# A hybrid RWKV-7 and latent-attention block: rotary parts of queries and key on GpSimd, and one PSUM bank copied out before a norm

## The chip, the cores and the metric

The kernel runs on one core of one Trainium2 chip, in one launch. A NeuronCore has five engines that each work through an instruction list of their own, in order: TensorE (PE in the profile, with PEld for its weight loads), VectorE (DVE), ScalarE (ACT), GpSimd (POOL) and SyncE (SP, which issues most of the loads). They meet only through semaphores. TensorE writes PSUM banks; the others work in SBUF and, all but GpSimd here, in PSUM. The metric is device time in microseconds for one execution of the program; the time of a kernel is the median of its runs.

## What is computed

One residual block over 256 tokens, width 2048, all float32. Cut to what matters here:

```python
u = rms_norm(h, pre_mix_norm)
z_rw, z_mla, z_gate = jnp.split(u @ w_in, ...)
y_rw = rwkv7_mixer(z_rw, ...)               # 16 heads x 64, state scan over time
cq, ckv, k_pe = jnp.split(z_mla, (512, 1024), axis=-1)
q  = (rms_norm(cq, q_norm) @ w_q_up).reshape(B, S, 8, 192)     # 128 plain + 64 rotary per head
kv = (rms_norm(ckv, kv_norm) @ w_kv_up).reshape(B, S, 8, 256)  # 128 key + 128 value per head
def rope(x, cos, sin):
    x1, x2 = jnp.split(x, 2, axis=-1)
    return jnp.concatenate([x1 * cos - x2 * sin, x2 * cos + x1 * sin], axis=-1)
q_pe = rope(q_pe, ...); k_pe = rope(k_pe, ...)                 # one key part for all heads
y_mla = block_causal_softmax(q, k) @ v
mix = (sigmoid(gA) * (y_rw @ Wa) + sigmoid(gB) * (y_mla @ Wb)) @ W_out
h = h + rms_norm(mix); h = h + rms_norm(gated_conv_mlp(h)); h = h + rms_norm(sigmoid(h @ W_pg) * (p @ W_ple))
```

The rotary step takes each vector of 64, swaps its two halves, and adds the original times cosine and the swapped one times plus or minus sine. The block needs it for eight query heads (four tiles of 128 rows: two heads in each) and for the one key part.

## The kernel before

**Products.** Activations are kept feature by feature: 128 features on the partitions, 256 tokens along the row. To keep float32 accuracy, each operand is cut into a high half (`hi`, rounded to the engine's fast float32 form) and a low half (`lo`, what is left), and three products are added: hi x hi, hi x lo, lo x hi (`fm3`, L183, L184, L185; `tm` with L196, L198 and L200 where tokens become the rows of the result, as for the values). A weight chunk is 128 x 1024 floats, 512 KB, loaded by SyncE into one of three `raw` buffers; `wchunk` cuts it in two steps of 512 columns, ScalarE making `hi` (L148) and VectorE making `lo` (L149), with five buffers of each. So every chunk that TensorE uses costs ScalarE two casts and VectorE two subtractions. A "duo" is a product with two times 128 output features into one PSUM bank (`d`); four such banks go round.

**The first 120 us.** Duos 1 to 4 of the input projection give the query latent and the key/value latent, each of 512 features. `latent` copies them out and sums their squares; `latent_norm` makes the reciprocal root on VectorE, spreads it over the partitions with two transposes on TensorE (`rs`, L377), scales each of the four 128-feature blocks (`latn`, L409) and splits the result into halves (`latm`, L161 on ScalarE and L162 on VectorE). Between them come a narrow product with the low-rank columns and the rotary key, and duos 0 and 5, the first RWKV parts; they are copied out by `evac` (L354), scaled by `rsb` (L368) and mixed with the token before (`rw_mix`, L361 and L362). Duo 5 is the last that uses `uT` without its norm factor; then `u_part` rewrites `uT` in four parts (L600 on VectorE, then L161 and L162), for all later RWKV duos.

Then come two duos with the rotary rows of the queries (w_q chunks 4 and 5), four value chunks (`dv0`, `dv1`, four times), the plain query and key duos of heads 0 and 1 (`upo`), and the attention of eight heads, two at a time, woven with further query, key and RWKV duos. The scores (`sc`) add a plain product (L637) and a rotary one (L638, `qp` with `kpe`).

**The rotary parts.** The query duo is copied to `o` (a tile named `upo`); ScalarE copies its four 32-partition quarters into `b` (`qps`) with neighbours exchanged (L610); VectorE multiplies `b` by sine (L612) and `o` by cosine into `a` (`qp`, L613) and adds (L614). For the key, VectorE writes the product with cosine into 64 partitions of each of two tiles `kpe` whose other halves are zero (L584), four products with minus sine into 32 partitions of `kp2` each (L586), and two sums (L588). The sign of sine for the first halves was folded into `sinT` before (L574).

**What sets the order.** The kernel's lines are recorded once; a tile framework then gives each engine its list, when the program is built, by priorities: lines written earlier go first where they can, the copies out of PSUM (`evac`, `rw_mix`) are raised, and work like `u_part` fills places in between. Engines never reorder at run time. Tiles of one tag share buffers in turn: `e1` has 5 of 256 columns and `e2` 17 of 512, and a new tile waits until the former owner of its buffer has been read for the last time. `kp2` takes the buffer of the broadcast `rb` of the second latent norm, which the transposes L377 read.

Of the kernel before, what the change touches and what calls it, by code (L numbers as in the profile page):

```python
# [11 lines left out]
AF = mybir.ActivationFunctionType  # L12
ALU = mybir.AluOpType
# [3 lines left out]
P = 128  # L17
T = 256
# [90 lines left out]
def hybrid_block(tc, A):  # L109
    nc = tc.nc  # L110
    es = ExitStack()
    mm = nc.tensor.matmul
    act = nc.scalar.activation
    tt = nc.vector.tensor_tensor
    ts = nc.vector.tensor_scalar
    stt = nc.vector.scalar_tensor_tensor

# [197 lines left out]
    def e1(nm, shape=None, dt=F32):  # L315
        return mp.tile(shape or [P, T], dt, name=nm, tag="e1", bufs=5)

    def e2(nm, shape=None, dt=F32):
        return mp.tile(shape or [P, 2 * T], dt, name=nm, tag="e2", bufs=17)
# [11 lines left out]
    def win_duo(i, ahead=None):  # L331
        return dense(umov, [A["w_in"][i, q] for q in range(4)], 4, ahead)

    def run(g):

        while True:
            try:
                next(g)
            except StopIteration as e:
                return e.value  # L340
# [11 lines left out]
    def evac(out, ps, **k):  # L352
        with tc.high_priority():
            act(out, ps, AF.Copy, **k)  # L354
# [8 lines left out]
                    op0=ALU.mult, op1=ALU.add)  # L363


    def scaled(out, ps, nb=2):
        evac(out, ps)
        tt(out=out, in0=out, in1=rsb[:].unsqueeze(1).to_broadcast([P, nb, T]), op=ALU.mult)  # L368

    def bcast(col, dst):  # L370
# [125 lines left out]
    cosT = mp.tile([P, T], F32, name="cosT")  # L496
    sinT = mp.tile([P, T], F32, name="sinT")
# [36 lines left out]
    lora = xn[:, 0, 0:3 * T].rearrange("p (b t) -> p b t", b=3)  # L534
    LM = zp.tile([P, 7, T], F32R, name="LM", bufs=1)
    akv = latent(lat[2:4])
    ps = run(dense(umov, [A["w_in1"][q] for q in range(2)], 8, cols=(0,)))
    rsb = mp.tile([P, T], F32, name="rsb")
    bcast(st[:, 6:8], rsb[:])
    cq = latent_norm(*aq, "q_norm")  # L540
    zs = e2("zs", [P, 2, T])
    scaled(zs[:, 0:1, :], ps[:, 0:1, :], 1)
    rw_mix(zs, 2, lora[:, 2:3, :], 1)
    zs = e2("zs", [P, 2, T])
    ps = run(win_duo(0))
# [1 line left out]
    rw_mix(zs, 0, lora[:, 0:2, :])  # L547

    zs = e2("zs", [P, 2, T])
    ps = run(win_duo(5))  # L550
    ckv = latent_norm(*akv, "kv_norm")
    scaled(zs[:], ps[:])
    zz = [[zp.tile([P, 2, T], F32, name="z0")], [], [], []]
    rw_mix(zs, 3, zz[0][0])
    act(lora[0:64, 0, :], lora[0:64, 0, :], AF.Tanh)
# [16 lines left out]
    Q = [slice(32 * i, 32 * i + 32) for i in range(4)]  # L572
# [5 lines left out]
    kpe = [mp.tile([P, T], F32, name=f"kpe{i}") for i in range(2)]  # L578
    kp2 = e1("kp2")
    key = lora[64:128, 2, :]  # L580
    for i in range(2):
        p = slice(64 * i, 64 * i + 64)
        nc.gpsimd.memset(kpe[i][64 - 64 * i:128 - 64 * i, :], 0.0)
        tt(out=kpe[i][p], in0=key, in1=cosT[64:128], op=ALU.mult)  # L584
        for x in range(2):
            stt(out=kp2[Q[2 * i + 1 - x]], in0=lora[Q[2 + x], 2, :], scalar=-1.0, in1=sinT[Q[2 + x]],  # L586
                op0=ALU.mult, op1=ALU.mult)
        tt(out=kpe[i][p], in0=kpe[i][p], in1=kp2[p], op=ALU.add)  # L588

    def up2(ap, lat):  # L590

# [13 lines left out]
    for j in range(2):  # L605
        ps = run(dense(cq, [A["w_q"][4 + j]], 4))
        o, b = e2("upo", [P, 2, T]), e2("qps", [P, 2, T])
        evac(o[:], ps[:])
        for i in range(4):
            act(b[Q[i ^ 1]], o[Q[i]], AF.Copy)  # L610
        a = mp.tile([P, 2, T], F32, name=f"qp{j}")
        tt(out=b[:], in0=b[:], in1=sinT[:].unsqueeze(1).to_broadcast([P, 2, T]), op=ALU.mult)  # L612
        tt(out=a[:], in0=o[:], in1=cosT[:].unsqueeze(1).to_broadcast([P, 2, T]), op=ALU.mult)  # L613
        tt(out=a[:], in0=a[:], in1=b[:], op=ALU.add)  # L614
        qp += [a[:, c, :] for c in range(2)]

    vt = [e2("vt") for _ in range(4)]
# [600 lines left out]
    with tc.tile_pool(name="fw", bufs=2) as fw, tc.tile_pool(name="psu", bufs=3, space=PSUM, reuse_waits="tile") as psu:  # L1218
# [30 lines left out]
        for n, (j, q) in enumerate([(j, q) for q in range(4) for j in range(3)] + [(j, q) for j in range(3, NFF) for q in range(4)]):  # L1249
            if q == 0:  # L1250
                pu[j] = psu.tile([P, 2, 512], F32, name="d")
            ps = pu[j]
# [193 lines left out]
```

## Time and profile before

| what | value |
|---|---|
| time, median of 3 runs | 1560.78 us (1560.56 to 1561.42) |
| profiled execution: time, span | 1560.39 us, 1558.6 us |
| TensorE busy, granted clock | 1538.0 us (99%), 0.997 |
| VectorE busy | 1182.2 us (76%) |
| ScalarE busy | 942.1 us (60%) |
| GpSimd busy | 60.9 us (4%) |
| loads | 281.16 MB read, 182 GB/s over the span |

The profiled execution's time is 1.8 us above its span, which runs from the first to the last instruction. Busy shares are means over the whole span; stages within it differ, and VectorE is much busier near 100 us than on average. In the profile's rows, a group reads: line, engine, operation, names of what it writes and reads, shape, count, then busy us and mean ns of one, then the engine's idle time before them and what ended it. A row of the timeline begins with start and length in us. Two operations of VectorE overlap by some 0.08 us in their recorded lengths when they run back to back.

### The profile page before, as it was taken

To read this page: it belongs to the slowest core of one execution; us is meant where nothing else is said; L and a number is where in the kernel's file an instruction comes from. 1 tells how busy PE (TensorE), PEld (TensorE's weight loads), DVE (VectorE), ACT (ScalarE), POOL (GpSimd) and SP (SyncE) were. 2 spreads that over 40 slices of the span, in tenths; PEclk is the share of its full clock that TensorE was granted. 3 is DMA by queue.
4 is the path that set the end of the run, shared out by engine and by line. 5 is a ranking of instruction groups with operands and counts; after the bars stand their busy time and mean duration, and the time that the engine had idled before them with its cause. 6 is when DMAs were issued, how large, how long until landed. Compare 5 with 4: busy or idle time off the path is not lost.

```text
span 1558.6 us, 29636 instructions
## 1 busy us (share of the span) xinstructions
PE 1538.0 (99%) x10850; PEld 1388.3 (89%) x10850; DVE 1182.2 (76%) x2670; ACT 942.1 (60%) x1944; POOL 60.9 (4%) x125
## 2 busy tenths in 40 slices
PE   9999999999999999999999999999999999999997
PEld 9989999999999999887888888888888888888886
DVE  7896687898989776557787777777777655777866
ACT  7686756566565555456766555555655555776653
POOL 0000201101011102000000000000000000000000
PEclk9999999999999999999999999999999999999998
DMA  8654555454444546865656555565655666666564
GB/s 304 192 172 141 154 173 164 138 171 129 147 150 136 160 153 200 306 199 167 203 174 205 198 181 202 179 203 179 206 181 190 175 192 195 197 197 191 166 200 148
DMA packets 80482, 285.19 MB, mean 183 GB/s; under 512 B 9040, under 2 KB 10320, under 8 KB 80336
## 3 DMA queue, kind: packets, MB, share of 16 engines
q1 hardware_dynamic: 77760, 279.48, 56.3%
q10 hardware_dynamic: 2576, 3.81, 0.7%
q8 instruction: 85, 1.39, 0.4%
q14 instruction: 61, 0.50, 0.1%
HBM read 281.16 MB, written 2.10 MB: 182 GB/s over the span
## 4 chain that ended last, share of the span: by engine, by line
PE 89%; DVE 6%; ACT 2%; DMA 1%; issue 1%; DVEq 0%; ACTq 0%
PE d L170 21%; PE d L174 11%; PE d L183 9%; PE d L185 8%; PE d L184 8%; PE o L196 7%; PE o L198 6%; PE o L200 6%; PE e L196 2%; PE e L198 2%; PE e L200 2%; DVE lo L149 2%; ACT hi L148 1%; DMA raw<-in_w_in 1%; PE tr L237 0%
## 5 line engine op out<-in xcount | busy, mean ns | idle before, releaser
L149 DVE TENSOR_TENSOR lo<-raw,hi 128x512 fp32r<-128x512 f32 x684 | 461.0, 690 | 213.9 <-ACT hi L148 208.5
L148 ACT CAST hi<-raw 128x512 fp32r<-128x512 f32 x684 | 410.7, 619 | 297.9 <-PE o L200 97.9
L183 PE MATMUL d<-uT,hi 128*128 128x256 f32 x1072 | 307.7, 287 | 0.7 <-ACT hi L161 0.6
L170 PE MATMUL d<-u,highs 128*128 128x512 f32 x1312 | 305.5, 390 | 0.0
L185 PE MATMUL d<-uT,lo 128*128 128x256 f32 x1072 | 300.5, 280 | 0.7 <-DVE lo L162 0.2
L184 PE MATMUL d<-uT,hi 128*128 128x256 f32 x1072 | 299.6, 279 | 0.1
L170 PEld LDWEIGHTS d<-u,highs 128*128 128x128 f32 x1312 | 243.3, 188 | 48.9
L148 ACT CAST highs<-raw 128x512 fp32r<-128x512 f32 x328 | 186.8, 616 | 115.0 <-DMA raw<-in_w_up 80.3
L183 PEld LDWEIGHTS d<-uT,hi 128*128 128x128 f32 x1072 | 201.7, 188 | 2.8 <-ACT hi L161 0.8
L185 PEld LDWEIGHTS d<-uT,lo 128*128 128x128 f32 x1072 | 201.5, 188 | 2.1 <-DVE lo L149 1.1
L184 PEld LDWEIGHTS d<-uT,hi 128*128 128x128 f32 x1072 | 201.7, 188 | 0.4 <-DVE uT L290 0.3
L149 DVE TENSOR_TENSOR hi<-raw,highs 128x512 fp32r<-128x512 f32 x164 | 112.7, 688 | 76.8 <-PE d L174 58.8
L174 PE MATMUL d<-u,lo 128*128 128x256 f32 x752 | 117.7, 280 | 0.0
L149 DVE TENSOR_TENSOR lo<-raw,highs 128x512 fp32r<-128x512 f32 x164 | 112.0, 684 | 0.0
L174 PE MATMUL d<-u,hi 128*128 128x256 f32 x656 | 103.3, 279 | 0.0
L174 PEld LDWEIGHTS d<-u,lo 128*128 128x128 f32 x752 | 101.7, 188 | 0.8
L174 PEld LDWEIGHTS d<-u,hi 128*128 128x128 f32 x656 | 91.5, 188 | 3.5
L198 PE MATMUL o<-lo,fsplit 128*128 128x512 f32 x264 | 88.6, 389 | 0.0
L196 PE MATMUL o<-hi,fsplit 128*128 128x512 f32 x264 | 88.5, 389 | 0.0
L200 PE MATMUL o<-hi,fsplit 128*128 128x512 f32 x264 | 88.4, 389 | 0.0
L1228 ACT ACTIVATE cy<-d 128x512 f32<-128x512 f32 x44 | 26.2, 597 | 67.8 <-PE d L174 67.8
L198 PEld LDWEIGHTS o<-lo,fsplit 128*128 128x128 f32 x264 | 49.6, 188 | 10.7 <-DVE lo L149 0.3
(389 smaller groups left out, 2550.9 us busy)
## 6 DMA issues: line engine op xcount, KB each, us to landing
raw<-in_w_up SPq DMA_DIRECT2D x176, 512.0 KB, 4.3
raw<-in_w_in SPq DMA_DIRECT2D x133, 512.0 KB, 3.6
raw<-in_w_down SPq DMA_DIRECT2D x88, 512.0 KB, 4.3
raw<-in_w_out SPq DMA_DIRECT2D x32, 512.0 KB, 4.4
raw<-in_w_pg SPq DMA_DIRECT2D x32, 512.0 KB, 3.6
raw<-in_w_bm SPq DMA_DIRECT2D x16, 512.0 KB, 3.7
raw<-in_w_br SPq DMA_DIRECT2D x16, 512.0 KB, 3.7
raw<-in_w_kv SPq DMA_DIRECT2D x8, 512.0 KB, 3.6
```

The costliest lines, as they stand in the source:

```text
L148: nc.scalar.copy(hi[:], raw[:, c:c + 512])
L149: tt(out=lo[:], in0=raw[:, c:c + 512], in1=hi[:].bitcast(F32), op=ALU.subtract)
L170: mm(ps[:, c, :], hi(i, col, P), mov[i][2], start=first and x == 0 and i == 0, stop=False)
L174: mm(ps[:, c, 0:T], lo(i, col, P), mov[i][0], start=False, stop=last and x == len(parts) - 1 and i == len(mov) - 1)
L183: mm(ps[:, c, :], hi(i, col, P), mov[i][:, 0:T], start=f, stop=False)
L184: mm(ps[:, c, :], hi(i, col, P), mov[i][:, T:2 * T], start=False, stop=False)
L185: mm(ps[:, c, :], lo(i, col, P), mov[i][:, 0:T], start=False, stop=l)
L196: mm(b[:], h, hi(i, g * 512, 512), start=f, stop=False)
L198: mm(b[:], h, lo(i, g * 512, 512), start=False, stop=False)
L200: mm(b[:], x, hi(i, g * 512, 512), start=False, stop=l)
L1228: act(y[:], ps[:, :, 0:T], AF.Copy)
```

## The change

All element-wise work of the rotary step goes from VectorE and ScalarE to GpSimd: for the key, two products with cosine, four with sine (now without the -1, and the sum became a subtraction), and two subtractions; for the queries, in each of two duos, four quarter copies, two products and a sum. And the copy of duo 5 out of its PSUM bank, which `scaled` made after the second `latent_norm`, is now written ahead of that norm; the scaling alone stays behind it.

```diff
+    gt = nc.gpsimd.tensor_tensor
...
-    def scaled(out, ps, nb=2):
-        evac(out, ps)
+    def scaled(out, ps=None, nb=2):
+        if ps is not None:
+            evac(out, ps)
         tt(out=out, in0=out, in1=rsb[:].unsqueeze(1).to_broadcast([P, nb, T]), op=ALU.mult)
...
     zs = e2("zs", [P, 2, T])
-    ps = run(win_duo(5))
+    evac(zs[:], run(win_duo(5))[:])
     ckv = latent_norm(*akv, "kv_norm")
-    scaled(zs[:], ps[:])
+    scaled(zs[:])
...
-        tt(out=kpe[i][p], in0=key, in1=cosT[64:128], op=ALU.mult)
+        gt(out=kpe[i][p], in0=key, in1=cosT[64:128], op=ALU.mult)
         for x in range(2):
-            stt(out=kp2[Q[2 * i + 1 - x]], in0=lora[Q[2 + x], 2, :], scalar=-1.0, in1=sinT[Q[2 + x]],
-                op0=ALU.mult, op1=ALU.mult)
-        tt(out=kpe[i][p], in0=kpe[i][p], in1=kp2[p], op=ALU.add)
+            gt(out=kp2[Q[2 * i + 1 - x]], in0=lora[Q[2 + x], 2, :], in1=sinT[Q[2 + x]], op=ALU.mult)
+        gt(out=kpe[i][p], in0=kpe[i][p], in1=kp2[p], op=ALU.subtract)
...
         for i in range(4):
-            act(b[Q[i ^ 1]], o[Q[i]], AF.Copy)
+            nc.gpsimd.tensor_copy(b[Q[i ^ 1]], o[Q[i]])
         a = mp.tile([P, 2, T], F32, name=f"qp{j}")
-        tt(out=b[:], in0=b[:], in1=sinT[:].unsqueeze(1).to_broadcast([P, 2, T]), op=ALU.mult)
-        tt(out=a[:], in0=o[:], in1=cosT[:].unsqueeze(1).to_broadcast([P, 2, T]), op=ALU.mult)
-        tt(out=a[:], in0=a[:], in1=b[:], op=ALU.add)
+        gt(out=b[:], in0=b[:], in1=sinT[:].unsqueeze(1).to_broadcast([P, 2, T]), op=ALU.mult)
+        gt(out=a[:], in0=o[:], in1=cosT[:].unsqueeze(1).to_broadcast([P, 2, T]), op=ALU.mult)
+        gt(out=a[:], in0=a[:], in1=b[:], op=ALU.add)
```

Lines behind the first added one count one or two higher in the changed kernel: L149 becomes L150, L161 and L162 become L162 and L163, L354 becomes L355, L409 becomes L411, L600 becomes L601.

The scheduler makes new lists of it. TensorE's keeps all its products in their order but for two transposes of the first attention, which go ahead of two steps of a duo (near 122 us); SyncE's is unchanged. GpSimd had nothing between the zeroing of `kpe` at the start and that of `Xb` at the end of the attention:

```order
L583 MEMSET kpe_1272 64x256
L583 MEMSET kpe_1273 64x256
L707 MEMSET Xb_2502 128x512
L707 MEMSET Xb_2503 128x512
L707 MEMSET kb_2504 128x512
```

Now these rows stand between them (ISA is the load of an instruction library, which stood ahead of the gate products before; `kpe` is the key's rotary part, `upo` the copied-out query duo, `qps` its exchanged quarters, `qp` the result):

```order
L586 ISA
L586 TENSOR_TENSOR kpe_1272<-xn,cosT 64x256
L588 TENSOR_TENSOR kp_1274<-xn,sinT 32x256 x3
...
L589 TENSOR_TENSOR kpe_1273<-kpe_1273,kp_1274 64x256
L611 COPY qps<-upo 32x512 x4
L614 TENSOR_TENSOR qp_1327<-upo,cosT 128x512
L613 TENSOR_TENSOR qps<-qps,sinT 128x512
L611 COPY qps<-upo 32x512
L615 TENSOR_TENSOR qp_1327<-qp_1327,qps 128x512
L611 COPY qps<-upo 32x512 x3
L614 TENSOR_TENSOR qp_1373<-upo,cosT 128x512
```

Eight key operations and fourteen query operations are all in GpSimd's list, in this order.

On VectorE, the stretch from the key's sums to the `lo` of the first chunk of the plain queries of heads 0 and 1 (the last row) read before:

```order
L586 SCALAR_TENSOR_TENSOR kp_1274<-xn,sinT 32x256
L149 TENSOR_TENSOR lo<-raw,hi 128x512
L588 TENSOR_TENSOR kpe_1272<-kpe_1272,kp_1274 64x256
L586 SCALAR_TENSOR_TENSOR kp_1274<-xn,sinT 32x256
L362 SCALAR_TENSOR_TENSOR z_1247<-zs,vec,z_1247 128x255 x2
L586 SCALAR_TENSOR_TENSOR kp_1274<-xn,sinT 32x256
L149 TENSOR_TENSOR lo<-raw,hi 128x512 x2
L588 TENSOR_TENSOR kpe_1273<-kpe_1273,kp_1274 64x256
L149 TENSOR_TENSOR lo<-raw,hi 128x512
L613 TENSOR_TENSOR qp_1327<-upo,cosT 128x512
L612 TENSOR_TENSOR qps<-qps,sinT 128x512
L149 TENSOR_TENSOR lo<-raw,hi 128x512
```

and reads now, up to the same `lo`:

```order
L163 TENSOR_TENSOR latm<-latn,latm 128x256
L370 TENSOR_TENSOR zs<-zs,rsb 128x512
L150 TENSOR_TENSOR lo<-raw,hi 128x512
L163 TENSOR_TENSOR uT<-xT,uT 128x2x256
L363 SCALAR_TENSOR_TENSOR z_1247<-zs,vec,z_1247 128x255 x2
L150 TENSOR_TENSOR lo<-raw,hi 128x512
L163 TENSOR_TENSOR uT<-xT,uT 128x2x256
L150 TENSOR_TENSOR lo<-raw,hi 128x512
L601 SCALAR_TENSOR_TENSOR xT<-xT,vec,rsb 128x256
L150 TENSOR_TENSOR lo<-raw,hi 128x512
L601 SCALAR_TENSOR_TENSOR xT<-xT,vec,rsb 128x256 x3
L150 TENSOR_TENSOR lo<-raw,hi 128x512
```

The rotary operations are gone, and parts of `u_part` (`xT` and `uT`) that stood behind this `lo` have taken their places.

On ScalarE, the copies out of PSUM around the second norm read before:

```order
L161 ACTIVATE latm<-latn 128x256
L148 CAST hi<-raw 128x512
L161 ACTIVATE latm<-latn 128x256
L354 ACTIVATE zs<-d 128x512
L354 ACTIVATE upo<-d 128x512
```

and now:

```order
L355 ACTIVATE zs<-d 128x512
L162 ACTIVATE uT<-xT 128x2x256
L149 CAST hi<-raw 128x512
L162 ACTIVATE latm<-latn 128x256 x3
L149 CAST hi<-raw 128x512 x2
L162 ACTIVATE latm<-latn 128x256
L355 ACTIVATE upo<-d 128x512
L149 CAST hi<-raw 128x512
```

`zs`, the copy of duo 5, has moved ahead of all four splits `latm`; `upo`, the copy of the first rotary duo, still stands behind the fourth.

## The prediction

> **What bounds the kernel now.** I read the page's busy shares first, then the busy time by stretch, then the waits of TensorE in the stretch that the change touches.
>
> ```profile
> PE 1538.0 (99%) x10850; PEld 1388.3 (89%) x10850; DVE 1182.2 (76%) x2670; ACT 942.1 (60%) x1944; POOL 60.9 (4%) x125
> ```
>
> TensorE (PE) is busy 1538.0 of 1558.6 us. Over the whole span VectorE (DVE) has a quarter of its time free and GpSimd (POOL) nearly all. That average is not what counts here; the stretch from 70 to 118 us is, where the rotary work runs:
>
> ```profile
> core 0: us, PE busy (x) PEld busy (x) DVE busy (x) ACT busy (x) POOL busy (x), PEclk, DMA share, GB/s
> 70.00:84.60 14.60, 14.60 (x126) 14.60 (x125) 13.63 (x29) 12.84 (x27) 0.00 (x0) 1.00 0.55 160
> 84.60:100.00 15.40, 13.72 (x85) 11.93 (x84) 15.13 (x32) 12.68 (x26) 0.00 (x0) 1.00 0.54 148
> 100.00:110.00 10.00, 10.00 (x72) 9.27 (x71) 9.83 (x18) 9.85 (x19) 0.00 (x0) 1.00 0.68 198
> 110.00:118.00 8.00, 7.60 (x59) 7.19 (x58) 7.85 (x24) 5.31 (x13) 0.00 (x0) 1.00 0.57 195
> ```
>
> From 84.6 to 110 us VectorE is busy 24.96 of 25.4 us: here it has no spare time, and it makes the low halves of all weights (`lo`, L149) without which TensorE cannot finish a chunk. The DMA share is 0.54 to 0.68, so loads are not the limit. The granted clock is 1.00. TensorE waits only three times from 84 to 123 us:
>
> ```profile
> PE dv L196 <- ACT zs L354: 1.7, 1, 1.7
> PE sc L637 <- ACT upo L354: 0.4, 1, 0.4
> PE pt L653 <- ACT s L647: 0.4, 1, 0.4
> ```
>
> So 1.7 us is what the second part of the change can win: a value product waits for the bank of the first RWKV duo, which ScalarE (ACT) copies out only behind the four splits of the second latent norm:
>
> ```profile
> 92.03 0.42 ACT L161 ACTIVATE latm<-latn 128x256 fp32r<-128x256 f32 x1 [0.40 <-DVE latn L409]
> 92.36 0.58 ACT L354 ACTIVATE zs<-d 128x512 f32<-128x512 f32 x1
> ...
> 90.92 0.39 PE L200 MATMUL dv<-hi,latm 128*128 128x512 f32 x1
> 92.99 0.50 PE L196 MATMUL dv<-hi,latm 128*128 128x512 f32 x1 [1.68 <-ACT zs L354]
> ```
>
> **The change part by part.** *The earlier copy.* In the new ScalarE order the copy stands ahead of the splits of `latn`, so the bank is free before 90.9 us and the 1.68 us go. The two waits of 0.4 us stay: they are the ends of chains (last product, copy or exponential, next product) that the change leaves as they are.
>
> *What ScalarE and VectorE lose.* The first of the key's products, and the groups of the stretch 84 to 114 us, price it:
>
> ```profile
> 71.91 0.42 DVE L584 TENSOR_TENSOR kpe<-xn,cosT 64x256 f32<-64x256 f32 x1
> ...
> L149 DVE TENSOR_TENSOR lo<-raw,hi 128x512 fp32r<-128x512 f32 x19 | 12.8, 686 | 0.3 <-ACT hi L148 0.2
> ...
> L600 DVE SCALAR_TENSOR_TENSOR xT<-xT,vec,rsb 128x256 f32<-128x256 f32 x8 | 3.6, 478 | 0.0
> ...
> L586 DVE SCALAR_TENSOR_TENSOR kp<-xn,sinT 32x256 f32<-32x256 f32 x4 | 1.7, 418 | 0.1
> L612 DVE TENSOR_TENSOR qps<-qps,sinT 128x512 f32<-128x512 f32 x2 | 1.4, 685 | 0.0
> L613 DVE TENSOR_TENSOR qp<-upo,cosT 128x512 f32<-128x512 f32 x2 | 1.4, 684 | 0.0
> L614 DVE TENSOR_TENSOR qp<-qp,qps 128x512 f32<-128x512 f32 x2 | 1.4, 684 | 0.0
> ...
> L588 DVE TENSOR_TENSOR kpe<-kpe,kp 64x256 f32<-64x256 f32 x2 | 0.8, 416 | 0.0
> ...
> L610 ACT ACTIVATE qps<-upo 32x512 f32<-32x512 f32 x8 | 5.0, 630 | 0.2
> ```
>
> VectorE loses 4 x 0.42 + 2 x 0.42 + 6 x 0.69 = 6.7 us here, and two products of the key (L584, 0.42 each) near 72 us. ScalarE loses 5.0 us. If nothing else changed, this relief could not be turned into time beyond the waits above, since TensorE waits for nothing else.
>
> *What GpSimd gains, and what one operation costs there.* In the window it did nothing before; now it does 22 operations: eight on the key with 256 elements a partition, then eight copies and six two-input operations with 512. The nearest rows:
>
> ```profile
> L930 POOL COPY av<-sv x8: 607/610/616, 268.4 to 540.1; 128x512 f32<-128x512 f32 x8
> ...
> L831 POOL COPY vw<-z x16: 391/532/761, 182.9 to 479.3; 64x256 f32<-64x256 f32 x16
> ...
> L797 POOL COPY bk<-bk x8: 454/522/2397, 205.6 to 471.7; 64x256 f32<-64x256 f32 x8
> ...
> 601.31 1.60 POOL L1090 TENSOR_TENSOR g<-g,mix 128x512 f32<-128x512 f32 x1 [3.94 <-DVE g L1089]
> ...
> 601.08 0.68 DVE L149 TENSOR_TENSOR lo<-raw,hi 128x512 fp32r<-128x512 f32 x1
> ```
>
> A copy of 512 elements takes 0.61 us, one of 256 elements 0.39 us at its shortest, but up to 0.76 and 2.40. Why so unequal? Because such a copy and a VectorE operation with two SBUF inputs hold each other up:
>
> ```profile
> 288.00 0.52 POOL L797 COPY bk<-bk 64x256 f32<-64x256 f32 x1 [2.09 <-DVE bk L791]
> ...
> 287.86 0.41 DVE L792 TENSOR_SCALAR a<-a,vec,oka 128x256 f32<-128x256 f32 x1
> 288.18 0.89 DVE L149 TENSOR_TENSOR lo<-raw,hi 128x512 fp32r<-128x512 f32 x1
> ...
> 478.18 0.76 POOL L831 COPY vw<-z 64x256 f32<-64x256 f32 x1
> ...
> 477.99 0.69 DVE L149 TENSOR_TENSOR lo<-raw,hi 128x512 fp32r<-128x512 f32 x1
> 478.60 0.62 DVE L800 SCALAR_TENSOR_TENSOR rk<-z,vec,kp 128x256 f32<-128x256 f32 x1
> ```
>
> At 288.00 the copy waits for the end of L792 (0.52 instead of 0.39, so it starts 0.14 before that operation's recorded end), and the `lo` behind it takes 0.89 instead of 0.69: 0.20 us longer, until 0.13 before the copy's end. At 478.18 the copy waits out a `lo`, then goes ahead of L800, which takes 0.62 where L600, of the same form, takes 0.48. So one waits for the other, whole operations at a time, and GpSimd mostly gets the next turn. By this, one GpSimd operation holds VectorE for its own length less 0.13 us. A 512-element copy holds it 0.48 us. The two-input operation at 601.31 waited for the `lo` that ended at 601.76, 0.31 us by the same 0.14; of its 1.60 us 1.29 are its own, and it holds 1.16. For the two-input form with 256 elements there is no row; it lies between the copy's 0.39 and 1.29, and by elements it is about 0.70, holding 0.57. No row shows VectorE waiting behind a two-input GpSimd operation: the bounds are 0 (it does not wait) and the 1.16 us; I take the second, because the same operation itself waited for VectorE as the copies do.
>
> The Trainium skill (the page "SBUF — State Buffer", section "Who interferes with whom") states this as a rule: an instruction of VectorE with two SBUF inputs contends with a GpSimd instruction that reads SBUF, and the second to issue fully blocks. The trace agrees where it has such pairs, with the 0.20 us at 288.18; the rule gives GpSimd every turn that it asks for first, and that case is priced among the rivals.
>
> *The sum, at one checkpoint.* I follow the `lo` of the first chunk of the first query duo, the last row of both VectorE excerpts above.
>
> ```profile
> 84.62 0.38 PE L377 MATMUL rs<-cst,rb 128*128 128x128 f32 x2
> ...
> 100.99 0.68 DVE L149 TENSOR_TENSOR lo<-raw,hi 128x512 fp32r<-128x512 f32 x1
> ...
> 103.83 0.28 PE L185 MATMUL d<-latm,lo 128*128 128x256 f32 x1
> ```
>
> It ends at 101.67 and is used at 103.83: a lead of 2.2 us. Of VectorE's own work ahead of it the change takes away the key's eight operations (8 x 0.42 = 3.4 us) and two of the query's (1.2 us; back to back, an operation starts 0.08 us before the recorded end of the one ahead, as at 478.60, so each of the two counts 0.60), 4.6 us. The scheduler fills this: six of the L600 (0.40 us each so counted, 2.4 us) and two splits of `uT` (1.2 us) have moved ahead of it, 3.6 us. The remaining 1.0 us pays for the two holds (2 x 0.57) near 72 us. So without collisions the `lo` comes when it came before. With them: the six later key operations start when the broadcast's transposes (L377, at 84.62) free their buffer, with eight two-input VectorE operations ahead of the value products' first `lo`; all six get a turn, 6 x 0.57 = 3.4 us. The fourteen query operations start when ScalarE has copied out the first rotary duo, now behind the fourth `latm`; fifteen VectorE operations then stand ahead of the checkpoint. Giving GpSimd two turns in three, ten get in: seven copies and three two-input operations, 7 x 0.48 + 3 x 1.16 = 6.8 us. Together 10.2 us, less the lead of 2.2: TensorE reaches the query duo about **8.0 us later** than now, with its 1.7 us wait no longer separate (it is inside this delay). The four operations that are left (4.0 us of holds) meet a VectorE that needs 0.6 us for each 1.4 us of TensorE; they add at most 0.4 each, and the relief of VectorE at the attention's start takes about as much back: nothing. After that TensorE has no slack to catch up (page: 99%), so the 8.0 us stay to the end. 1560.39 of the profiled execution + 8.0 = 1568.4; the median of the three runs is 0.4 above the profiled time: **1568.8 us**.
>
> What is behind it: `lo` waits, so the products wait; the buffers of `hi` and `lo` come free later, so the loads behind them start later, at a DMA share that leaves room. Nobody else waits for GpSimd before the first scores,
>
> ```profile
> 110.92 0.38 PE L637 MATMUL sc<-upo 128*128 128x128 f32 x1 [0.40 <-ACT upo L354]
> ```
>
> and these need only the first query tile, which by then is done or nearly so. GpSimd's library load moves from the gate products to the program's start, where GpSimd then waits until about 70 us for the key: nothing.
>
> **The rivals.** *No collision with the two-input form, or a VectorE that is not delayed.* Then the 1.7 us wait is the whole effect: 1560.8 - 1.7 = 1559.1 us. For it: no row shows the opposite for that form, and the lead of 2.2 us covers the 1.7 us. Against it: the 0.20 and 0.14 us at 288.18 and 478.60. This is the case on the other side; it decides if VectorE's rows keep their lengths beside GpSimd's. Chance 0.14, of which I give 0.05 to a gain above 0.2%.
>
> *VectorE keeps the turn.* One episode shows it:
>
> ```profile
> 205.61 2.40 POOL L797 COPY bk<-bk 64x256 f32<-64x256 f32 x1 [12.35 <-DVE bk L791]
> ...
> 207.06 0.68 DVE L149 TENSOR_TENSOR lo<-raw,hi 128x512 fp32r<-128x512 f32 x1
> 207.66 0.47 DVE L362 SCALAR_TENSOR_TENSOR z<-d,vec,z 128x255 f32<-128x255 f32 x1
> ```
>
> That copy got in only at L362, which reads PSUM. Then `lo` is hardly late, but the first query tile, with seven GpSimd operations between its bank's copy and the scores at 111 us, gets through only in gaps. Its 4 x 0.48 + 3 x 1.16 = 5.4 us of holds must find room in the 20 us in which VectorE has a few PSUM operations and about 1 us of idle time; about 4 us are missing, half of them paid by TensorE at the scores and half by `lo`, less the 1.7: about +2, 1562.8 us. Chance 0.22; the median 0.52 of the L797 copies against their maximum of 2.40 speaks against it as the rule.
>
> *GpSimd gets every turn, or its forms cost more* (32 partitions moved to another quadrant are in no row). All twenty holds ahead of the checkpoint are 3.4 + 8 x 0.48 + 6 x 1.16 = 14.2 us, less 2.2: +12.0, 1572.8 us. Chance 0.15.
>
> *The change does not do what it says:* excluded for the copy, whose place in ScalarE's order has moved; the operations of the rotary parts do stand on GpSimd.
>
> **How the numbers follow.** Two turns in three: 0.49, with 1565 to 1572 as its own range. A measurement of this kernel tells 0.2% (3.1 us) from no change. Slower by more: 0.49 + 0.15 + 0.06 (of the 0.22) = 0.70. Within: 0.16 + 0.09 = 0.25. Faster by more: 0.05. The range from 1561 to 1574 us takes in the second rival and the every-turn case and leaves out the case without collisions and a tail above.
>
> **What would show it.** In the changed kernel's rows, `lo` (L150) between 85 and 115 us should have a mean well over 686 ns, with single ones near 1.2 to 1.9 us beside GpSimd's two-input operations; GpSimd's 512-element copies a good deal over 0.61; TensorE should wait for DVE `lo` several times from 88 to 115 us, 8 us or so in all, and no longer for `zs`; the first scores should start near 119 us instead of 110.9. I am wrong if `lo` keeps its 0.69 us (no collision), or if GpSimd's operations stretch and VectorE's do not (VectorE keeps the turn), when the wait should be at the scores for GpSimd.

## The result, and the profile after

The changed kernel takes 1572.54 us, median of its runs (1572.02 to 1573.57), beside 1560.94 for the kernel before: a ratio of 1.0072 with a 95% interval of 1.0059 to 1.0085. The change costs 11.6 us; 8.0 were forecast, in a range from 1561 to 1574.

The profiled execution took 1572.23 us, 11.84 more than the one before. The waits of TensorE from 60 to 140 us in the changed kernel (engine and operation, who is waited for, us in all, times, longest):

```profile
PE d L186 <- DVE lo L150: 3.5, 2, 2.9
PE dv L199 <- DVE lo L150: 2.1, 3, 1.1
PE dv L197 <- ACT latm L162: 2.0, 1, 2.0
PE dv L201 <- DVE latm L163: 0.5, 1, 0.5
```

The wait for `zs` is gone. Five waits for `lo` and two for the second latent have come, 8.1 us together. VectorE's groups from 84 to 125 us, and GpSimd's from 60 to 130 us (count, busy us, mean ns of one):

```profile
L150 DVE TENSOR_TENSOR lo<-raw,hi 128x512 fp32r<-128x512 f32 x21 | 19.0, 920 | 3.3 <-ACT hi L149 3.2
L163 DVE TENSOR_TENSOR uT<-xT,uT 128x512 fp32r<-128x512 f32 x6 | 7.2, 1206 | 0.0
L601 DVE SCALAR_TENSOR_TENSOR xT<-xT,vec,rsb 128x256 f32<-128x256 f32 x6 | 6.3, 1092 | 0.0
```
```profile
L611 POOL COPY qps<-upo 32x512 f32<-32x512 f32 x8 | 7.0, 877 | 5.7 <-ACT upo L355 5.3
L588 POOL TENSOR_TENSOR kp<-xn,sinT 32x256 f32<-32x256 f32 x4 | 4.1, 1014 | 13.0 <-PE rs L379 12.8
L615 POOL TENSOR_TENSOR qp<-qp,qps 128x512 f32<-128x512 f32 x2 | 3.2, 1619 | 0.2
L613 POOL TENSOR_TENSOR qps<-qps,sinT 128x512 f32<-128x512 f32 x2 | 3.2, 1599 | 0.0
L614 POOL TENSOR_TENSOR qp<-upo,cosT 128x512 f32<-128x512 f32 x2 | 2.7, 1334 | 0.2
```

`lo` had a mean of 686 ns, L600 (now L601) of 478. How the two engines take turns is seen in the timeline of the changed kernel, first VectorE, then GpSimd (start, length):

```profile
100.19 1.78 DVE L150 TENSOR_TENSOR lo<-raw,hi 128x512 fp32r<-128x512 f32 x1
101.89 1.78 DVE L163 TENSOR_TENSOR uT<-xT,uT 128x512 fp32r<-128x512 f32 x1
103.59 1.09 DVE L150 TENSOR_TENSOR lo<-raw,hi 128x512 fp32r<-128x512 f32 x1
104.61 1.51 DVE L601 SCALAR_TENSOR_TENSOR xT<-xT,vec,rsb 128x256 f32<-128x256 f32 x1
...
109.97 1.75 DVE L150 TENSOR_TENSOR lo<-raw,hi 128x512 fp32r<-128x512 f32 x1
```
```profile
100.07 1.35 POOL L614 TENSOR_TENSOR qp<-upo,cosT 128x512 f32<-128x512 f32 x1
101.37 1.75 POOL L613 TENSOR_TENSOR qps<-qps,sinT 128x512 f32<-128x512 f32 x1
103.18 0.95 POOL L611 COPY qps<-upo 32x512 f32<-32x512 f32 x1
104.22 1.62 POOL L615 TENSOR_TENSOR qp<-qp,qps 128x512 f32<-128x512 f32 x1
```

One VectorE operation, one GpSimd operation, and so on. A `lo` with a copy ahead of it takes 1.09 instead of 0.69 (0.40 held), one with a two-input operation ahead of it 1.78 (1.09 held). The last VectorE row is the `lo` of the checkpoint, the first chunk of the first query duo. It ends at 111.72, against 101.67 before, and its product starts at 111.78, against 103.83: 7.95 us later.

From there on the forecast said "nothing". TensorE in the changed kernel, at the checkpoint and at the first scores:

```profile
111.78 0.39 PE L186 MATMUL d<-latm,lo 128*128 128x256 f32 x1 [2.92 <-DVE lo L150]
114.08 0.58 PE L186 MATMUL d<-latm,lo 128*128 128x256 f32 x1 [0.61 <-DVE lo L150]
122.14 0.49 PE L638 MATMUL sc<-upo 128*128 128x128 f32 x2
```

The first scores stood at 110.92 and stand at 122.14: 11.22 us later. So 3.3 us came in the ten us behind the checkpoint: 10.36 us from the one to the other, 7.09 before. Two things are seen there. The first is the granted clock, in the changed kernel's busy time by stretch, cut where the clock changes (length, PE, PEld, DVE, ACT and POOL busy, then PEclk):

```profile
92.82:96.23 3.41, 2.93 (x7) 2.16 (x7) 3.41 (x9) 2.26 (x6) 0.04 (x1) 0.50 0.42 150
...
113.30:116.72 3.42, 2.81 (x14) 2.65 (x13) 3.42 (x7) 0.46 (x1) 0.00 (x0) 0.50 0.43 129
116.72:120.13 3.41, 3.41 (x18) 3.41 (x17) 1.52 (x3) 1.73 (x3) 0.00 (x0) 0.50 0.81 246
```

It falls to a half twice, behind the waits of 2.0 and 2.92 us, the second time for some 7 us. The second is the load of the first key and value chunk, for which a cast on ScalarE waits:

```profile
114.05 0.33 SPq L142 DMA_DIRECT2D raw<-in_w_kv  x1
```
```profile
117.69 0.62 ACT L149 CAST hi<-raw 128x512 fp32r<-128x512 f32 x1 [3.93 <-DMA raw<-in_w_kv]
```

Before, that load was issued at 103.51, just ahead of the checkpoint; now it is issued 2.3 us behind it, when VectorE has released one of the three `raw` buffers. After the first scores 0.6 us come back (10.62 at 126 us) and 1.0 goes again, in small steps from 180 us on (11.66 at 1352 us).

### The profile page after: what moved, and what is told of

The parts are those of the page before. It is cut to its first block, busy times and chain, and to the rows that moved or that the text cites. A ratio compares the mean times of both kernels' runs of the same rounds, so it can differ in the third digit from the quotient of the medians.

```text
span 1570.2 us, 29645 instructions
## 1 busy us (share of the span) xinstructions
PE 1543.6 (98%) x10850; PEld 1391.7 (89%) x10850; DVE 1188.6 (76%) x2656; ACT 936.5 (60%) x1936; POOL 84.4 (5%) x147
## 4 chain that ended last, share of the span: by engine, by line
PE 89%; DVE 7%; ACT 2%; DMA 1%; issue 1%; DVEq 0%; ACTq 0%
PE d L171 20%; PE d L175 10%; PE d L184 9%; PE d L186 8%; PE d L185 8%; PE o L199 6%; PE o L197 6%; PE o L201 6%; DVE lo L150 2%; PE e L197 2%; PE e L199 2%; PE e L201 2%; ACT hi L149 1%; DMA raw<-in_w_in 1%; DVE xT L601 1%
## 5 line engine op out<-in xcount | busy, mean ns | idle before, releaser
L150 DVE TENSOR_TENSOR lo<-raw,hi 128x512 fp32r<-128x512 f32 x684 | 466.8, 698 | 218.2 <-ACT hi L149 212.1
L149 ACT CAST hi<-raw 128x512 fp32r<-128x512 f32 x684 | 410.2, 619 | 305.2 <-PE o L201 99.3
L149 ACT CAST highs<-raw 128x512 fp32r<-128x512 f32 x328 | 186.7, 616 | 117.5 <-DMA raw<-in_w_up 86.4
L150 DVE TENSOR_TENSOR hi<-raw,highs 128x512 fp32r<-128x512 f32 x164 | 112.8, 689 | 78.7 <-PE d L175 59.5
L150 DVE TENSOR_TENSOR lo<-raw,highs 128x512 fp32r<-128x512 f32 x164 | 112.1, 685 | 0.0
```

The costliest lines, as they stand in the source:

```text
L149: nc.scalar.copy(hi[:], raw[:, c:c + 512])
L150: tt(out=lo[:], in0=raw[:, c:c + 512], in1=hi[:].bitcast(F32), op=ALU.subtract)
```

## The experiments

Each ratio is to runs of the kernel before on the same chip, with its 95% interval; 0.001 is 1.56 us. "Checkpoint" and "scores" are the starts of the first `lo` product of the first query duo and of the first scores in the profiled execution.

| kernel | ratio | checkpoint, us | scores, us |
|---|---|---|---|
| before | 1 | 103.83 | 110.92 |
| the change | 1.0072 (1.0059 to 1.0085) | 111.78 | 122.14 |
| copy_only | 1.0000 (0.9991 to 1.0009) | 101.80 | 110.48 |
| rotary_only | 1.0071 (1.0055 to 1.0086) | 109.93 | 121.22 |
| key_only | 1.0021 (1.0011 to 1.0031) | 107.37 | 115.57 |
| query_only | 1.0058 (1.0044 to 1.0071) | 112.51 | 121.61 |
| writes_only | 0.9980 (0.9971 to 0.9989) | 101.85 | 109.20 |
| copies_only | 1.0019 (1.0009 to 1.0028) | 104.07 | 112.88 |
| fill | 1.0079 (1.0064 to 1.0094) | 112.03 | 121.82 |
| own_buf | 1.0080 (1.0067 to 1.0094) | 115.88 | 124.17 |
| fill_own | 1.0085 (1.0071 to 1.0099) | 115.32 | 122.95 |

**The earlier copy alone.** The kernel before with only this:

```diff
-    ps = run(win_duo(5))
+    evac(zs[:], run(win_duo(5))[:])
     ckv = latent_norm(*akv, "kv_norm")
-    scaled(zs[:], ps[:])
+    scaled(zs[:])
```

> Only the bank of the first RWKV duo is copied out earlier; the rotary work stays on VectorE and ScalarE as before. Theory (the loss comes from GpSimd and VectorE taking turns): the 1.68 us wait for zs goes and no hold comes, so 1560.9 - 1.7 = about 1559.2 us. Rival (the earlier copy itself upsets the order, as the wait of 2.0 us for the fourth latm in the changed kernel could suggest): as slow as before or slower, 1561 to 1563 us.

Measured: 1.0000. The theory missed. The time is at the rival's lower end, as slow as before, but for another reason than an upset order: TensorE reaches the checkpoint 2.03 us earlier and the scores only 0.44 earlier, since there a new wait stands. TensorE and ScalarE in this kernel:

```profile
108.55 0.28 PE L183 MATMUL d<-latm,hi 128*128 128x256 f32 x1
...
108.81 1.12 ACT L148 CAST hi<-raw 128x512 fp32r<-128x512 f32 x2
...
109.83 0.59 ACT L354 ACTIVATE upo<-d 128x512 f32<-128x512 f32 x1
...
110.48 0.49 PE L638 MATMUL sc<-upo 128*128 128x128 f32 x2 [1.65 <-ACT upo L354]
```

The copy of the key duo stands behind two casts in ScalarE's list, and the scores behind the copy. The 1.68 us wait for `zs` has become a 1.65 us wait for `upo` (0.40 before), and by 126 us the lead is 0.0. What the second part of the change removes was not the last wait of this stretch.

**The rotary work alone**, the bank copied out where it was. To the changed kernel:

```diff
-    evac(zs[:], run(win_duo(5))[:])
+    ps = run(win_duo(5))
     ckv = latent_norm(*akv, "kv_norm")
-    scaled(zs[:])
+    scaled(zs[:], ps[:])
```

> All rotary work on GpSimd, the bank copied out where it was before. Theory: the 1.7 us wait lies inside the delay that the turns make, so nearly all of the loss stays: 1571 to 1574 us. Rival (the two edits only hurt together, by the new order): 1561 to 1565 us.

Measured: 1.0071, as the change. All of the loss is in the rotary part; the theory held.

**The key alone and the queries alone**, each with the earlier copy; the other part of the rotary work is as before. To the changed kernel:

```diff
-            nc.gpsimd.tensor_copy(b[Q[i ^ 1]], o[Q[i]])
+            act(b[Q[i ^ 1]], o[Q[i]], AF.Copy)
...
-        gt(out=a[:], in0=a[:], in1=b[:], op=ALU.add)
+        tt(out=a[:], in0=a[:], in1=b[:], op=ALU.add)
```

so for key_only, with the two products likewise, and for query_only

```diff
-        gt(out=kpe[i][p], in0=key, in1=cosT[64:128], op=ALU.mult)
+        tt(out=kpe[i][p], in0=key, in1=cosT[64:128], op=ALU.mult)
...
-        gt(out=kpe[i][p], in0=kpe[i][p], in1=kp2[p], op=ALU.subtract)
+        tt(out=kpe[i][p], in0=kpe[i][p], in1=kp2[p], op=ALU.add)
```

with the products with sine as before.

> The earlier copy and the key's eight operations on GpSimd; the queries' rotary work on VectorE and ScalarE as before. Theory (GpSimd gets every turn, each holds VectorE for its own length): TensorE meets the late lo of the value products by about 2 to 4 us, and finds ScalarE 5 us fuller than in the changed kernel; 1561 to 1565 us, with no VectorE row lengthened after about 97 us. Rival (the key's operations end before anything is tight): 1559 us.

> The earlier copy and the queries' fourteen operations on GpSimd; the key stays on VectorE. Theory: ahead of the first query duo's lo all ten to fourteen get their turn, 8 x 0.48 + 6 x 1.16 = 10.8 us at most, less 1.2 us of VectorE's own work saved and the lead of 2.2 us: 5 to 8 us, and more if the granted clock falls behind the waits; 1565 to 1570 us. Rival (the key's part did it): 1559 to 1561 us.

Measured: 1.0021 and 1.0058, at the upper end of what was expected of each. Together they are 1.0079, near the change's 1.0072, so the two losses add up within their intervals. That the holds add up is not shown by this, for how the queries alone lose their part was not foreseen. ScalarE in query_only:

```profile
97.59 0.62 ACT L149 CAST hi<-raw 128x512 fp32r<-128x512 f32 x1 [0.30 <-PE dv L201]
109.70 0.63 ACT L162 ACTIVATE uT<-xT 128x512 fp32r<-128x512 f32 x1 [11.49 <-DVE xT L602]
110.24 1.12 ACT L149 CAST hi<-raw 128x512 fp32r<-128x512 f32 x2
111.27 1.07 ACT L355 ACTIVATE vt<-dv 128x512 f32<-128x512 f32 x2
```

One split of `uT` waits 11.5 us for a late VectorE operation, and behind it in ScalarE's list wait the copies of the value banks; TensorE needs one of these banks for the query duo and stands for 6.0 us. Behind the two waits below the clock falls as well, for 3.4 and 6.8 us:

```profile
PE d L184 <- ACT vt L355: 6.0, 1, 6.0
PE dv L199 <- DVE lo L150: 2.2, 1, 2.2
```

**GpSimd writes only.** Every rotary operation of the change becomes one memset of what it wrote (two for each two-input operation of the queries):

```diff
-            nc.gpsimd.tensor_copy(b[Q[i ^ 1]], o[Q[i]])
+            nc.gpsimd.memset(b[Q[i ^ 1]], 0.0)
...
-        gt(out=b[:], in0=b[:], in1=sinT[:].unsqueeze(1).to_broadcast([P, 2, T]), op=ALU.mult)
+        nc.gpsimd.memset(b[:], 0.0)
+        nc.gpsimd.memset(b[:], 0.0)
...
+        nc.gpsimd.memset(a[:], 0.0)
```

> The changed kernel, with each GpSimd rotary operation replaced by memsets of the same tile that take about as long (a copy by one, a two-input query operation by two or three): the rotation of queries and key is left out. GpSimd is as busy and as late as in the changed kernel, and the order of all other engines is nearly the same, but it reads nothing from SBUF. Theory (what holds VectorE up is GpSimd reading SBUF beside VectorE's two-input operations): lo keeps its 0.69 us, no wait for DVE lo, granted clock 1.00, 1558 to 1560 us. Rival (the new order of the engines, or GpSimd being late): 1570 us or more. Second rival (any GpSimd access to SBUF holds VectorE, writes too): 1565 us or more with lengthened lo.

Measured: 0.9980, faster. VectorE from 84 to 112 us, then GpSimd from 60 to 125 us:

```profile
L150 DVE TENSOR_TENSOR lo<-raw,hi 128x512 fp32r<-128x512 f32 x21 | 14.3, 693 | 2.9 <-ACT hi L149 2.8
```
```profile
L611 POOL MEMSET qps<- 32x512 f32 x8 | 4.2, 519 | 0.3
L588 POOL MEMSET kp<- 32x256 f32 x4 | 1.2, 304 | 77.9 <-DVE uT L163 77.8
L613 POOL MEMSET qps<- 128x512 f32 x2 | 1.1, 530 | 0.1
L614 POOL MEMSET qps<- 128x512 f32 x2 | 1.1, 526 | 0.1
```

The memsets wait for less than the operations did: those of `qp` and `kpe` ran near the program's start, and 7.6 us of them beside the busy VectorE. There `lo` keeps 693 ns, and the six `lo` that run beside the memsets, from 85 to 93 us, take 0.68 to 0.69 us each. So these writes hold nobody up; what holds VectorE is that GpSimd reads SBUF. And nearly the same order of VectorE, ScalarE and TensorE is 0.2% faster than before, 3.1 us (1.7 to 4.5), so the new order is not the cause. That the order would also be harmless with GpSimd late is not tested here; the changed kernel has no wait for GpSimd.

The scores come 1.72 us earlier than before, the 125th us 2.29 earlier. That is what the early copy and the relief of VectorE (6.7 us) and ScalarE (5.0 us) are worth together when nothing is held up; the early copy alone gave 0.44 at the scores and nothing at 125 us. In the profiled execution 1.3 of the 2.29 us are lost again from 250 to 350 us; why stays open.

**The quarter copies alone** on GpSimd, with the earlier copy; all arithmetic stays on VectorE. To copy_only:

```diff
-            act(b[Q[i ^ 1]], o[Q[i]], AF.Copy)
+            nc.gpsimd.tensor_copy(b[Q[i ^ 1]], o[Q[i]])
```

> The earlier copy, and of the rotary work only the eight quarter copies of the queries on GpSimd; all arithmetic stays on VectorE. Theory (price by operation): eight copies of one input hold VectorE 8 x 0.48 = 3.8 us at most, less the lead of 2.2 us: 0 to +2 on the kernel with the earlier copy alone, 1559 to 1561.5 us, and no fall of the granted clock. Rival (any GpSimd traffic costs the same, whatever its length; or it is the change of place between quadrants that is dear): 1564 us or more.

Measured: 1.0019, some 3 us: above the theory's 0 to 2 and at the edge of the rival's range, which began 3.1 us above the kernel before. Up to the checkpoint the theory's price holds: 104.07 against 101.80 with the early copy alone, 2.3 us for 8 copies of 0.40, less some slack. So the rival's reasons don't hold: the price is not the same for every form (0.40 here, 1.09 with two inputs), and the change of place is not dear. The rest comes behind it: a wait of 2.0 us for `upo` at the scores, behind which the granted clock falls to a half (113 to 117 us). The "no fall" of the expectation was wrong.

**What a pause of TensorE costs.** The kernel before, with a product, so many memsets of 0.2 us on GpSimd, and a second product that waits for them; the rest of the attention is queued behind. One pause ahead of the third pair of heads (near 148 us; the expectation's "first scores" is wrong) for idle_s and idle_m, three, ahead of pairs two to four and with 6, 7 and 8 memsets, for idle_steps. With 5 memsets (12 in idle_m):

```diff
+            mm(pz[:, 0:P], wt[:], wt[:], start=True, stop=True)
+            for _ in range(5):
+                nc.gpsimd.memset(wt[:], 0.0)
+            i2 = mm(pz[:, P:2 * P], wt[:], wt[:], start=True, stop=True)
```

> The kernel before, with a pause put ahead of the first scores: a 128x128 product, 5 memsets on GpSimd (0.2 us each) that wait for it, and a second product that waits for them. TensorE waits about 1.2 us once. Theory (a wait of about 2 us or more makes the granted clock fall to a half for some us; a shorter one doesn't): clock 1.00 after it, the time is the wait and the two products, +1.0 to +1.8 us: 1562 to 1563 us. Rival (the fall after the waits of the changed kernel was chance or came from VectorE's lateness): the same here.

> The same with 12 memsets: a wait of about 2.6 us. Theory: the granted clock then falls to a half for 3 to 7 us, which loses half of that stretch in work: +2.6 + 1.7 to 3.5 and the products 0.3: 1565 to 1567.5 us. Rival (chance, or VectorE's lateness): the wait alone, 1563.5 to 1564 us at a granted clock of 1.00.

> The kernel before with three pauses ahead of the scores of the second, third and fourth pair of heads, by 6, 7 and 8 memsets on GpSimd: waits of about 1.6, 1.9 and 2.1 us, tens of us apart. Theory (a bound between 1.8 and 2.0 us): granted clock 1.00 after the first, 0.50 for some 3.4 us after the third, the second open; 5.6 us of waits, 0.9 us of products, 1.7 to 3.4 us lost at half clock: 1569 to 1572 us. Rival (no sharp bound; the fall depends on the moment): any of the three, the first too, or none.

Measured: ratios of 1.0016 (1.0007 to 1.0026), 1.0037 (1.0024 to 1.0051) and 1.0064 (1.0048 to 1.0081). The waits were 1.38 us; 3.2 us; and 1.64, 1.96 and 2.21 us. The busy time by stretch, cut at the clock's own steps of 3.41 us (the last section shows them), of idle_steps behind its three pauses and of idle_m behind its one:

```profile
131.73:135.15 3.42, 3.42 (x32) 3.42 (x31) 2.23 (x9) 2.36 (x8) 0.00 (x0) 1.00 0.04 14
...
152.21:155.63 3.42, 3.42 (x17) 3.42 (x17) 1.51 (x7) 0.84 (x4) 0.00 (x0) 0.50 0.12 48
...
176.11:179.52 3.41, 3.41 (x18) 3.41 (x18) 1.67 (x8) 1.53 (x6) 0.00 (x0) 0.50 0.00 0
```
```profile
152.55:155.96 3.41, 3.41 (x18) 3.41 (x17) 1.60 (x8) 1.07 (x5) 0.00 (x0) 0.50 0.00 0
```

No fall behind 1.38 and 1.64 us; a fall for some 3.4 us behind 1.96, 2.21 and 3.2 us. At the pause the products behind it fell back by 2.1 us in idle_s and by 5.5 us in idle_m: 3.4 us more, of which 1.8 are the longer wait and the rest, 1.6, half of a stretch of some 3.4 us. So the fall follows the wait, whoever makes TensorE wait. In total idle_s lost more than expected, since the stretch from 250 to 350 us became 2.1 us longer in its profiled execution; why stays open, and others of these kernels move there by up to 1.3 us.

A sharp bound on the length of a wait does not hold. Of the waits from 1.77 to 2.2 us between 84 and 180 us in all these kernels (one of 1.80 us in rotary_only, which began at half clock, left out) ten are followed by a fall and two are not: 2.05 us near 96 us in own_buf, and this one in fill, behind which the clock stays at 1.00:

```profile
121.82 0.49 PE L642 MATMUL sc<-upo 128*128 128x128 f32 x2 [2.08 <-ACT upo L359]
```

None of 1.7 us or less is followed by one, and each of 2.9 us or more is. What sets the two apart from the ten is where the wait lies on a grid of 3.41 us; the last section shows it.

**The last 3.3 us: the clock or the load?** First the clock. The changed kernel with 20 repeats of one product inside the 2.92 us wait, so that TensorE is not idle there; no other instruction moves (`fill` holds the number 20 once, at this place):

```diff
+                for _ in range(fill.pop() if fill else 0):
+                    mm(ps[:, c, :], hi(i, col, P), mov[i][:, 0:T], start=True, stop=True)
                 mm(ps[:, c, :], hi(i, col, P), mov[i][:, 0:T], start=f, stop=False)
```

> The changed kernel with 20 products more ahead of the first of the first query duo: the same first product, repeated, each overwriting the one before (about 0.12 us each, 2.3 us in all). They fill most of the 2.92 us in which TensorE waits there for DVE lo; no other instruction moves on any engine. Theory (a wait of 2 us or more makes the granted clock fall to a half, and the 6.9 us at half clock from 113 us on are the last 3.5 us of the loss): the clock stays at 1.00 after it, and in spite of 2.3 us more work the time falls by about 3.5 us, to 1569 us. Rival (the fall has another cause, or its loss is hidden): 1572.5 us or more.

Measured: 1.0079, no faster than the change. The clock did as expected; in fill:

```profile
114.00:116.00 2.00, 1.66 (x14) 1.66 (x15) 2.00 (x4) 0.00 (x1) 0.00 (x0) 1.00 0.45 63
116.00:118.00 2.00, 2.00 (x20) 2.00 (x19) 1.30 (x3) 0.05 (x1) 0.00 (x0) 1.00 0.82 236
```

But TensorE, at full clock, now waits 2.08 us at the scores: the cast of the key chunk starts at 117.95 as it did at 117.69, for its load is as late as before. The theory that the half clock is the last 3.5 us falls. It lies beside the late load, and either holds the scores.

So the load gets a buffer of its own, once with the wait as it is and once with it filled (`own` is true for this chunk alone):

```diff
-            raw = wp.tile([P, WC], F32, name="raw", bufs=3)
+            own = bool(owns and owns.pop())
+            raw = mp.tile([P, WC], F32, name="raw1") if own else wp.tile([P, WC], F32, name="raw", bufs=3)
```

> The changed kernel, with a weight buffer of its own for the chunk of the first key and value duo, whose load (issued at 114.05 us, landed 117.6) waited in the changed kernel for VectorE to release one of three buffers. No product is added, so TensorE still waits about 2.9 us for lo and then runs at half clock for some 7 us. Theory (late load and half clock lie beside each other, either alone holds the scores): ratio to the kernel before 1.006 to 1.0075, as the change. Rival (the load alone is the cause): 1.004 to 1.0055.

> The same buffer of its own, and the 20 repeated products in the wait for lo. Load early and clock whole: theory (the two together are the last 3.2 us): first scores near 119 us and ratio 1.0045 to 1.0058, about 1569 to 1570 us on a kernel before of 1561 to 1562. Rival (the scores are late for a third reason, such as ScalarE's order): 1.007 or more.

Measured: 1.0080 and 1.0085. By its time alone fill_own speaks for a third reason, and by the profile there is one, but not at the scores. With a buffer to itself the load went to the program's start, to 0.73 us, and changed the order of loads and operations there; TensorE's first `uT` product came at 8.46 us (own_buf) and 8.98 us (fill_own) instead of 5.31; both kernels reach the checkpoint 3.5 to 4.1 us later for that. From the checkpoint to the scores:

| kernel | clock whole | load early | us from checkpoint to scores |
|---|---|---|---|
| before | yes | yes | 7.09 |
| the change | no (6.8 us at half) | no | 10.36 |
| fill | yes | no | 9.79 |
| own_buf | no (3.4 us at half) | yes | 8.29 |
| fill_own | yes | yes | 7.63 |

Both cured, 2.7 of the 3.3 us are gone; what is left, 0.5, is about the 0.63 us wait for the second `lo`, which stands behind the `uT` that GpSimd's last operation holds up. The scores of fill_own come 0.8 us behind the change's, having been 3.5 behind at the checkpoint. The half clock alone (fill) is worth 0.6 us here and the load alone (own_buf) 2.1, but own_buf also had a shorter stretch at half clock, 3.4 us instead of 7, so the two aren't cleanly apart. None of the three is a faster kernel; that the cures would save 2.7 us of the whole time was not measured.

## Why the prediction was right, and where it was not

**Right: the mechanism, the place and most of the size.** GpSimd operations that read SBUF and VectorE operations with two SBUF inputs took turns, whole operations at a time; `lo` rose from 686 to 920 ns, the waits moved to `lo` (5.6 of the 8.1 us; 2.5 are for the second latent), and the checkpoint came 7.95 us later where 8.0 had been worked out. That these two agree so closely is luck, as the next paragraph shows. writes_only shows that it is the reading, key_only and query_only that both halves of the rotary work pay. The rival "no collision" is out. Its 1.7 us gain would not have come from the copy alone (copy_only: nothing) but from the copy and the relief together: writes_only is 2.29 us ahead at the 125th us, and the three waits that the prediction listed make 2.5. So its sentence that the relief "could not be turned into time beyond the waits above" is not contradicted, and the 3.1 us of that run's ratio, with an interval from 1.7, don't settle it.

**"Giving GpSimd two turns in three, ten get in": wrong, by errors that nearly cancel.** It got every turn, thirteen of fourteen ahead of the end of the checkpoint's `lo`. That was the last rival, with a chance of 0.15; that its 1572.8 us is so near the 1572.5 measured is chance, since its 14.2 us of holds were not there and 3.3 us came from elsewhere. For each turn was cheaper than priced: 0.40 for a copy (0.48), 1.09 for a two-input operation (1.16), and the six key operations from 84.6 us on together 3.1 us (priced 3.4; seven VectorE operations, from 84.40 to 91.33, take 6.9 us and by their own lengths 3.8). The prediction's own figures explain this: a GpSimd operation starts 0.14 us before the recorded end of the VectorE operation ahead of it, where VectorE's next would have started 0.08 before it. So 0.06 us of each GpSimd operation lie beside work that VectorE does anyway, and the lengths of 0.61, 1.29 and 0.70 that it went by, less 0.13 and 0.06, give 0.42, 1.10 and 0.51. The queries' holds are 8 x 0.40 + 5 x 1.09 = 8.7 by these prices, and 8.4 in the rows from 96.66 to 111.65; 6.8 were forecast. Together 11.5 us, not 10.2. The checkpoint's `lo` was late by 10.05: some 1.4 us were absorbed, and candidates are VectorE's 0.4 us of idle time before, the 0.6 us that TensorE was ahead at 84 us in the execution after, and the 1.0 us set aside for two holds near 70 us, of which the rows show one, of 0.5. How they share it isn't settled.

The Trainium skill (the page "SBUF — State Buffer", section "Who interferes with whom") gives the turn to whichever instruction asks first and lets it block the other fully. The trace agrees: with both lists full the two engines alternate one by one. The hold near 70 us is of an operation with a single SBUF input: `TENSOR_SCALAR xn<-xn` takes 0.75 to 0.78 us beside the key's products on GpSimd in all six kernels that have these there, and 0.28 in the other eight. So operations with two SBUF inputs are not the only ones that are held.

**"They add at most 0.4 each, and the relief [...] takes about as much back: nothing": the step that failed.** Behind the checkpoint 3.3 us were lost. The prediction had seen that "the loads behind them start later, at a DMA share that leaves room" and priced it at nothing; but it is not bandwidth that ran out, it is the third buffer, which VectorE releases, so that the load's 3.6 us lie between VectorE's lateness and the scores. And it had no term for the clock, which it had read as 1.00 in every stretch. fill, own_buf and fill_own show the two causes of the way from the checkpoint to the scores; what each is worth in the whole time is not shown.

**The 1.7 us of the earlier copy.** In the prediction they lie inside the larger delay, and so it was. The size was wrong even alone: copy_only gains nothing, since the wait moves to `upo`.

**The scores "near 119".** They stand at 122.14: the 8.0 us plus what the failed step left out.

## What to carry to other kernels

Work given to an idle engine is not free if it and the engine that it relieves hold each other up at SBUF: here each GpSimd operation that read SBUF held VectorE for 0.4 to 1.1 us, and VectorE was the engine with no spare time in that stretch. So engines do not "meet only through semaphores", as is said at the start: these two also met at SBUF. Look for who is behind the waiting operation in each in-order list, and which buffer it will release: most of the loss behind the checkpoint (2.1 of 3.3 us by own_buf) came from a load that waited for a buffer, not for bandwidth. When a wait goes, find the next one in the same stretch before counting the gain, and when two causes lie beside each other, curing one can show little (fill: 0.6 of 3.3 us).

## What the hardware did that was not expected

The granted clock falls to a half behind waits of TensorE that are short: for 3.4 us behind a wait of about 2 us (twice that in rotary_only, where a wait of 1.80 us follows inside it), for 6.8 us behind 2.92 us followed by 0.61. Each such stretch costs half its length, if nothing else is later. A wait of 1.7 us costs itself; one of 2.0 us costs nearly twice that, ten times out of twelve. The Trainium skill ("TensorE: Matmul & The Clock Gate", section "Why this matters for your kernels") advises no gaps above about 3 us between bursts of products; here 1.77 us was enough:

```profile
93.25 0.50 PE L196 MATMUL dv<-hi,latm 128*128 128x512 f32 x1 [1.77 <-ACT zs L354]
```

This is the wait for `zs` in idle_m, with the clock at 0.50 from 94.5 to 97.9 us, while the same wait in the profiled execution before, 1.68 us, left it at 1.00.

The same page of the Trainium skill (section "What's actually happening") has the activity counted in windows of 3.4 us that run freely. The traces agree: in all fourteen the granted clock changes only at steps of a grid of 3.41 us, which begins at another moment in each execution. Here the busy time is cut at that grid, for idle_m, for the kernel before, and for fill around its 2.08 us wait:

```profile
91.11:94.52 3.41, 1.64 (x7) 1.05 (x6) 3.32 (x8) 2.98 (x7) 0.00 (x0) 1.00 0.75 195
94.52:97.94 3.42, 3.42 (x10) 2.67 (x9) 3.32 (x8) 3.37 (x7) 0.00 (x0) 0.50 0.32 117
```
```profile
89.78:93.19 3.41, 1.73 (x12) 1.26 (x11) 3.38 (x9) 2.61 (x7) 0.00 (x0) 1.00 0.57 163
93.19:96.60 3.41, 3.41 (x16) 2.73 (x16) 3.29 (x8) 3.36 (x8) 0.00 (x0) 1.00 0.56 159
```
```profile
117.37:120.78 3.41, 2.36 (x21) 2.17 (x19) 1.38 (x2) 1.76 (x4) 0.00 (x0) 1.00 0.86 261
120.78:124.20 3.42, 2.38 (x20) 2.38 (x21) 2.21 (x7) 2.00 (x5) 0.00 (x0) 1.00 0.64 205
124.20:127.61 3.41, 3.41 (x25) 3.20 (x24) 1.80 (x8) 2.05 (x6) 0.00 (x0) 1.00 0.46 148
```

In idle_m TensorE is idle for 1.77 us of the first window, and the next one runs at half clock; in the kernel before it is idle for 1.68, and the clock stays. In fill an edge of the grid cuts the wait into two parts of about 1.05 us, and it costs no clock; the 2.05 us in own_buf are cut likewise, and with the waits beside them the two windows have 1.07 and 1.53 us of idle time. Over the whole of the fourteen traces, up to the last products, each of the 15 full-clock windows with 1.77 us of idle time or more is followed by half clock, and none with 1.75 us or less is. So what tells the two kinds apart is the idle time within one window (as the profile models the ends of products), and not the length of a wait. The way back has a bound of its own: 15 half-clock windows with 0.48 us of idle time or less are followed by full clock, three with 0.61 or more by another at half. One of these three is the changed kernel's window from 113.30 us, with its 0.61 us wait; that is why its second stretch lasts for two windows.
